# Binary cross-entropy with 8-bit targets on one core: slots of 15232 columns, a larger first chunk, tail chunks loaded in turn, and whole-chunk clip, logarithm and negation

## The chip, the cores and the metric

The kernel runs on one core of one Trainium2 chip. The metric is the device time of one execution in microseconds (us). Times of the same kernel are taken in several runs; a profiled execution adds a trace with the start and the length of every instruction and every DMA packet. The engines that matter here are DVE (VectorE), ACT (ScalarE), POOL (GpSimd, which in this kernel only issues DMAs) and SP (SyncE, which issues the last stores). The core's 16 DMA engines move the data.

## The reference

Inputs are `pred` and `target`, both 8192 x 8192 in fp32; targets are 0 or 1.

```python
eps = 1e-7
pred = np.clip(pred, eps, 1 - eps)
return -(target * np.log(pred) + (1 - target) * np.log(1 - pred))
```

Both inputs are 268.4 MB, and so is the output. Since a target is 0 or 1, the kernel takes one logarithm an element: -ln|target - 1 + pred| is -ln(pred) for target 1 and -ln(1 - pred) for target 0.

## The kernel before, in words

The 67,108,864 elements are seen as one flat array, cut into chunks that are 128 partitions high and `w` columns wide. A chunk of `w` columns is contiguous in memory, and each partition holds one contiguous row of 4w bytes. There are 524288 columns in all: a first chunk of 5120 (chunk 0), 33 chunks of 15360 (`WIDE`, chunks 1 to 33), and a tail of three chunks of 5632, 5632 and 1024. In the code `z` is the number of the last wide chunk, 33; the tail is `z + 1`, `z + 2`, `z + 3`, here also called a, b and c.

Predictions lie in `ring_p`, three slots of 15360 fp32 columns; chunk k uses slot k mod 3, and the tail shares one slot. All work is done in place there, and the result is stored from there. Targets lie in `ring_t`, which has one slot of 15360 columns of 8 bits: the DMA reads fp32 from HBM and writes uint8. So targets k+1 can be loaded only when the merge of chunk k has read targets k.

A chunk goes through these steps, each a helper with a line of its own in the profile:

- `load_p` (L70): the prediction's DMA, from POOL's queue (chunk 0 from ACT's)
- `load_t` (L73): the target's DMA, from POOL's queue
- `clip` (L85): DVE TENSOR_SCALAR, max and min with the two bounds
- `merge`: DVE SCALAR_TENSOR_TENSOR (L91), target - 1 + pred, then on ACT the absolute value (L94) and the logarithm (L95)
- `negate` (L99): DVE TENSOR_SCALAR, times -1
- `store` (L79): the result's DMA, from POOL's queue up to chunk z - 1, from SP's queue from chunk z on. The last chunk's store is cut into three DMAs of 108, 12 and 8 rows

The order of instructions on every engine is written out by hand (`tc.manual_schedule()`); waits between engines follow from the data. An engine takes its instructions strictly in the order of the program, so an instruction that waits holds up all behind it on that engine, and the same holds for the DMA issues of POOL and SP. In an iteration of the main loop, clip, merge and negate work on two halves of a chunk (7680 columns each): merge of both halves of chunk k, the issue of targets k+1, negation of both halves, clip of both halves of chunk k+1, the issue of store k, the issue of predictions k+2. The last iteration issues the predictions of all three tail chunks there. After the loop chunk z is merged, the three target loads of the tail are issued, and the tail's steps are interleaved with the negation of chunk z.

Of the kernel before, what the change touches and what calls it, by code (L numbers as in the profile page):

```python
# [1 line left out]

# [4 lines left out]

EPS = 1e-7

WIDE = 15360  # L10
SLOTS = 3
TAIL = (5632, 5632, 1024)
ROWS = (108, 12, 8)


@with_exitstack
def kernel(
    ctx: ExitStack,
    tc: tile.TileContext,
    pred: bass.AP,  # L20
    target: bass.AP,
    out: bass.AP,
):
    nc = tc.nc
    fp32 = mybir.dt.float32
    low = mybir.dt.uint8
    Alu = mybir.AluOpType
    Act = mybir.ActivationFunctionType
    P = nc.NUM_PARTITIONS

    R, C = pred.shape
    total = R * C // P
    rest = total - sum(TAIL)
    n = rest // WIDE
    first = rest - n * WIDE
    assert 0 < first <= WIDE and n > 4 and sum(TAIL) <= WIDE
    spots = [(first, 0)]
    spots += [(WIDE, k % SLOTS * WIDE) for k in range(1, n + 1)]
    c = (n + 1) % SLOTS * WIDE
    for w in TAIL:  # L40
        spots.append((w, c))
        c += w
    n = len(spots)
    z = n - 1 - len(TAIL)
    starts = [sum(w for w, _ in spots[:k]) * P for k in range(n)]

    pool = ctx.enter_context(tc.tile_pool(name="rings", bufs=1))
    ring_p = pool.tile([P, SLOTS * WIDE], fp32, name="ring_p", tag="ring_p")
    ring_t = pool.tile([P, WIDE], low, name="ring_t", tag="ring_t")
    warm = pool.tile([1, 8], fp32, name="warm", tag="warm")  # L50

    def chunk(ap, k):
        flat = ap.rearrange("r c -> (r c)")
        w = spots[k][0]
        return flat[starts[k] : starts[k] + w * P].rearrange("(p w) -> p w", p=P)

    def cols(ring, k, part, c):
        w = spots[k][0]
        i, m = part
        return ring[:, c + i * w // m : c + (i + 1) * w // m]  # L60

    def p_of(k, part=(0, 1)):
        return cols(ring_p, k, part, spots[k][1])

    def t_of(k, part=(0, 1)):
        return cols(ring_t, k, part, spots[k][1] % WIDE)

    def load_p(k):
        queue = nc.scalar if k == 0 else nc.gpsimd
        queue.dma_start(out=p_of(k), in_=chunk(pred, k))  # L70

    def load_t(k):
        nc.gpsimd.dma_start(out=t_of(k), in_=chunk(target, k))  # L73

    def store(k):
        queue = nc.sync if k >= z else nc.gpsimd
        r = 0
        for rows in ROWS if k == n - 1 else (P,):
            queue.dma_start(out=chunk(out, k)[r : r + rows, :], in_=p_of(k)[r : r + rows, :])  # L79
            r += rows  # L80
        assert r == P

    def clip(k, *part):
        p = p_of(k, *part)
        nc.vector.tensor_scalar(  # L85
            out=p, in0=p, scalar1=EPS, scalar2=1 - EPS, op0=Alu.max, op1=Alu.min
        )

    def merge(k, *part):
        p, t = p_of(k, *part), t_of(k, *part)  # L90
        nc.vector.scalar_tensor_tensor(  # L91
            out=p, in0=t, scalar=1.0, in1=p, op0=Alu.subtract, op1=Alu.add
        )
        nc.scalar.activation(out=p, in_=p, func=Act.Abs)  # L94
        nc.scalar.activation(out=p, in_=p, func=Act.Ln)  # L95

    def negate(k, *part):
        p = p_of(k, *part)
        nc.vector.tensor_scalar(out=p, in0=p, scalar1=-1.0, scalar2=None, op0=Alu.mult)  # L99

    halves = (0, 2), (1, 2)
    tail = range(z + 1, n)
    with tc.manual_schedule():
        load_p(0)
        load_t(0)
        load_p(1)
        nc.vector.memset(warm, 1.0)  # L107
        nc.scalar.activation(out=warm, in_=warm, func=Act.Ln)  # L108
        for h in halves:
            clip(0, h)  # L110
        for k in range(z):
            for h in halves:
                merge(k, h)
            load_t(k + 1)
            for h in halves:
                negate(k, h)
            for h in halves:
                clip(k + 1, h)
            store(k)
            for j in (k + 2,) if k + 2 <= z else tail if k + 2 == z + 1 else ():  # L120
                load_p(j)
        for h in halves:
            merge(z, h)
        for j in tail:
            load_t(j)
        negate(z, halves[0])
        for j in tail:
            clip(j)
        merge(z + 1)
        negate(z, halves[1])  # L130
        store(z)
        merge(z + 2)
        negate(z + 1)
        store(z + 1)
        merge(z + 3)
        negate(z + 2)
        store(z + 2)
        negate(z + 3)
        store(z + 3)


# [1 line left out]
_INS = ['pred', 'target']  # L143
_OUTS = [((8192, 8192), 'float32')]


# [23 lines left out]
```

## Time and profile before

| what | us |
|---|---|
| median of 3 runs (lowest to highest) | 1877.95 (1876.52 to 1878.27) |
| the profiled execution's own time | 1878.45 |
| its span, from the first to the last instruction | 1876.2 |
| DVE busy | 1116.7 |
| ACT busy | 900.3 |
| POOL busy | 277.6 |
| merge on DVE, 7680 columns, one | 8.154 |
| clip or negation on DVE, 7680 columns, one | 4.158 and 4.160 |
| absolute value or logarithm on ACT, 7680 columns, one | 6.595 and 6.603 |

All 16 DMA engines together moved data at a busy share of 9 tenths or more in 39 of 40 equal slices of the span. The DMA issues on POOL take 0.53 us at the least and 4.09 us at the most.

In the views, a line of the timeline gives the start and the length in us, the engine, the line of the kernel, the operation, the names it writes and reads, how often it follows in a row, and in brackets how long the engine sat idle before it and what ended that. POOL's DMA_DIRECT2D is the issue of a DMA (the writing of its descriptors), not the transfer. In a line of the stretches of time, the length of the stretch is followed by the busy time of DVE, ACT and POOL, the granted clock, the DMA's busy share and the GB/s that it moved. A line of the chain of waits gives a start, a length and what the chain went through in that time.

### The profile page before, as it was taken

The numbers are of one execution on the slowest core, as the hardware profiler recorded it, in microseconds if no ns is written. First come the engines' busy times: TensorE is split into PE (matmuls) and PEld (weight loads), VectorE is DVE, ScalarE is ACT, GpSimd is POOL, SyncE is SP. The second block draws the span as 40 slices with busy tenths as digits, with TensorE's granted clock in tenths as the row PEclk, the third lists the DMA queues.
The fourth block names the chain that finished last, engine by engine and source line by source line (L and its number), as shares of the span: only waits on it lengthen the run. The fifth ranks groups of instructions, "written<-read, shape, count | busy, mean of one in ns | idle before, by whom it ended". The sixth has DMA issues, their size and how long they took to land.

```text
span 1876.2 us, 663 instructions
## 1 busy us (share of the span) xinstructions
DVE 1116.7 (60%) x214; ACT 900.3 (48%) x144; POOL 277.6 (15%) x110
## 2 busy tenths in 40 slices
DVE  4566665565566556556655655666566566655655
ACT  2555333555543355553335555444455544445554
POOL 0011111110111111011111101111111011111100
DMA  9999999999999999999999999999999999999998
GB/s 274 271 351 341 309 299 312 303 339 360 347 309 307 309 301 333 361 354 312 313 303 307 319 360 359 324 307 309 307 312 351 360 340 305 309 308 309 338 334 314
DMA packets 16004, 604.02 MB, mean 322 GB/s; under 512 B 1792, under 2 KB 1920, under 8 KB 2560
## 3 DMA queue, kind: packets, MB, share of 16 engines
q0 software_dynamic: 15264, 587.21, 97.6%
q1 hardware_dynamic: 592, 14.16, 1.8%
q10 hardware_dynamic: 144, 2.62, 0.4%
q14 instruction: 4, 0.03, 0.0%
HBM read 536.87 MB, written 268.44 MB: 429 GB/s over the span
## 4 chain that ended last, share of the span: by engine, by line
DMA 67%; issue 28%; DVE 2%; ACT 2%; POOL 0%; POOLq 0%; DVEq 0%; PEldq 0%
DMA ring_t<-in_target_dram 67%; DVE ring_p L91 2%; ACT ring_p L95 1%; ACT ring_p L94 1%; DVE ring_p L99 0%; POOL ring_p L70 0%; POOL out_dram L79 0%; DVEq L165 0%; POOLq L73 0%; POOLq L79 0%; DVEq L91 0%; PEldq L165 0%
## 5 line engine op out<-in xcount | busy, mean ns | idle before, releaser
L94 ACT ACTIVATE ring_p<-ring_p 128x7680 f32<-128x7680 f32 (+3 forms) x71 | 450.8, 6349 | 954.1 <-DVE ring_p L91 954.1
L91 DVE SCALAR_TENSOR_TENSOR ring_p<-ring_t,ring_p 128x7680 f32<-128x7680 uint8 (+3 forms) x71 | 554.3, 7846 | 251.4 <-DMA ring_t<-in_target_dram 251.4
L99 DVE TENSOR_SCALAR ring_p<-ring_p 128x7680 f32<-128x7680 f32 (+3 forms) x71 | 284.3, 4006 | 470.6 <-ACT ring_p L95 470.6
L95 ACT ACTIVATE ring_p<-ring_p 128x7680 f32<-128x7680 f32 (+3 forms) x71 | 451.3, 6356 | 2.3
L85 DVE TENSOR_SCALAR ring_p<-ring_p 128x7680 f32<-128x7680 f32 (+3 forms) x71 | 281.3, 4003 | 19.9 <-DMA ring_p<-in_pred_dram 19.9
L79 POOL DMA_DIRECT2D out_dram<-ring_p x33 | 125.1, 3791 | 711.5 <-DVE ring_p L99 711.5
L73 POOL DMA_DIRECT2D ring_t<-in_target_dram x37 | 19.7, 532 | 818.8 <-DVE ring_p L91 818.1
L70 POOL DMA_DIRECT2D ring_p<-in_pred_dram x36 | 132.9, 3692 | 0.0
L108 ACT ACT_TABLE_LOAD x1 | 1.3, 1283 | 1.1 <-PEq L154 1.1
L107 DVE MEMSET warm<- 1x8 f32 x1 | 0.1, 65 | 0.8 <-PEq L154 0.8
L108 ACT ACTIVATE warm<-warm 1x8 f32<-1x8 f32 x1 | 0.2, 207 | 0.0
L154 POOL MEMSET const-float32-0.0<- 128x1 f32 x1 | 0.1, 98 | 0.2 <-issue 0.2
L154 POOL MEMSET const-bfloat16-1.0<- 128x1 bf16 x1 | 0.1, 101 | 0.0
L154 POOL MEMSET const-float32-1.0<- 128x1 f32 x1 | 0.1, 98 | 0.0
L154 POOL MEMSET const-uint8-127<- 128x1 uint8 x1 | 0.1, 98 | 0.0
## 6 DMA issues: line engine op xcount, KB each, us to landing
ring_p<-in_pred_dram POOLq DMA_DIRECT2D x33, 7680.0 KB, 47.6
out_dram<-ring_p POOLq DMA_DIRECT2D x32, 7680.0 KB, 33.4
ring_t<-in_target_dram POOLq DMA_DIRECT2D x33, 1920.0 KB, 37.8
out_dram<-ring_p SPq DMA_DIRECT2D x1, 7680.0 KB, 19.7
ring_p<-in_pred_dram POOLq DMA_DIRECT2D x2, 2816.0 KB, 37.5
out_dram<-ring_p SPq DMA_DIRECT2D x2, 2816.0 KB, 16.0
ring_p<-in_pred_dram ACTq DMA_DIRECT2D x1, 2560.0 KB, 13.3
out_dram<-ring_p POOLq DMA_DIRECT2D x1, 2560.0 KB, 30.0
```

The source lines that it names most:

```text
L70: queue.dma_start(out=p_of(k), in_=chunk(pred, k))
L73: nc.gpsimd.dma_start(out=t_of(k), in_=chunk(target, k))
L79: queue.dma_start(out=chunk(out, k)[r : r + rows, :], in_=p_of(k)[r : r + rows, :])
L85: nc.vector.tensor_scalar(out=p, in0=p, scalar1=EPS, scalar2=1 - EPS, op0=Alu.max, op1=Alu.min)
L91: nc.vector.scalar_tensor_tensor(out=p, in0=t, scalar=1.0, in1=p, op0=Alu.subtract, op1=Alu.add)
L94: nc.scalar.activation(out=p, in_=p, func=Act.Abs)
L95: nc.scalar.activation(out=p, in_=p, func=Act.Ln)
L99: nc.vector.tensor_scalar(out=p, in0=p, scalar1=-1.0, scalar2=None, op0=Alu.mult)
L107: nc.vector.memset(warm, 1.0)
L108: nc.scalar.activation(out=warm, in_=warm, func=Act.Ln)
L154: nc = _bacc.Bacc("TRN2", target_bir_lowering=False, num_devices=1)
```

## The change

The slots become 15232 columns wide, and the tail 6208, 6208 and 1024. There are again 33 wide chunks; what is left for chunk 0 is 8192 columns. `merge` no longer takes the logarithm; a new helper `log` does. The clip becomes one instruction a chunk everywhere. Logarithm and negation become one instruction a chunk too, but for chunk 1 and chunk z, which keep halves. In the tail, the predictions' loads move behind the merges of chunk z in the program, and each is followed by its targets' load, so POOL issues p(a), t(a), p(b), t(b), p(c), t(c). The tail's steps get a new order: the second negation and the store of chunk z come ahead of all merges of the tail, and the negation of a stays behind the merge of b, that of b behind the merge of c.

```diff
-WIDE = 15360
+WIDE = 15232
 SLOTS = 3
-TAIL = (5632, 5632, 1024)
+TAIL = (6208, 6208, 1024)
...
         nc.scalar.activation(out=p, in_=p, func=Act.Abs)
+
+    def log(k, *part):
+        p = p_of(k, *part)
         nc.scalar.activation(out=p, in_=p, func=Act.Ln)
...
-        for h in halves:
-            clip(0, h)
+        clip(0)
         for k in range(z):
             for h in halves:
                 merge(k, h)
+                if k == 1:
+                    log(k, h)
             load_t(k + 1)
-            for h in halves:
-                negate(k, h)
-            for h in halves:
-                clip(k + 1, h)
+            if k == 1:
+                for h in halves:
+                    negate(k, h)
+            else:
+                log(k)
+                negate(k)
+            clip(k + 1)
             store(k)
-            for j in (k + 2,) if k + 2 <= z else tail if k + 2 == z + 1 else ():
-                load_p(j)
+            if k + 2 <= z:
+                load_p(k + 2)
         for h in halves:
             merge(z, h)
-        for j in tail:
+            log(z, h)
+        a, b, c = range(z + 1, n)
+        for j in a, b, c:
+            load_p(j)
             load_t(j)
         negate(z, halves[0])
-        for j in tail:
-            clip(j)
-        merge(z + 1)
+        clip(a)
         negate(z, halves[1])
         store(z)
-        merge(z + 2)
-        negate(z + 1)
-        store(z + 1)
-        merge(z + 3)
-        negate(z + 2)
-        store(z + 2)
-        negate(z + 3)
-        store(z + 3)
+        merge(a)
+        log(a)
+        clip(b)
+        merge(b)
+        log(b)
+        negate(a)
+        store(a)
+        clip(c)
+        merge(c)
+        log(c)
+        negate(b)
+        store(b)
+        negate(c)
+        store(c)
```

More of the change, by code (lines that the diff above doesn't have):

```diff
@@ L101 @@
     halves = (0, 2), (1, 2)
-    tail = range(z + 1, n)
     with tc.manual_schedule():
```

## The prediction

> **What bounds the kernel now.** I read the page first, then the time by shape, the timeline of the first 120 us and the last 130 us, narrow windows, and the chain in order of time. The page:
>
> ```profile
> DVE 1116.7 (60%) x214; ACT 900.3 (48%) x144; POOL 277.6 (15%) x110
> ...
> DMA  9999999999999999999999999999999999999998
> ...
> HBM read 536.87 MB, written 268.44 MB: 429 GB/s over the span
> ```
>
> No engine is full; the DMA is, in every slice. The chain shows its pace:
>
> ```profile
> 171.89 38.10 DMA ring_t<-in_target_dram
> ...
> 226.60 38.43 DMA ring_t<-in_target_dram
> ...
> 281.65 38.14 DMA ring_t<-in_target_dram
> ...
> 991.84 37.69 DMA ring_t<-in_target_dram
> ...
> 1698.32 37.73 DMA ring_t<-in_target_dram
> ...
> 1752.66 37.76 DMA ring_t<-in_target_dram
> ```
>
> One chunk's target load is issued per line. The last two stand 54.34 us apart, and in a chunk 3 x 7.864 MB cross HBM (prediction in, target in, result out): 434 GB/s, so a transfer of 15360 columns takes 18.12 us, 1.180 ns a column, whatever its kind. From 171.89 to 991.84 fifteen periods average 54.66, 0.32 over that; from there on nothing is over. The packet records show why: at first the sixteen DMA engines pass from one transfer to the next almost together, and the last target rows then take 0.3 to 0.5 us too long; later they have drifted 3 us apart and the rows take 2.28 us throughout.
>
> The bytes don't change, so the change can act only on time in which the DMA does nothing or is slow. It does nothing in two places:
>
> ```profile
> 93.49 8.23 DVE L85 TENSOR_SCALAR ring_p<-ring_p 128x7680 f32<-128x7680 f32 x2
> 93.87 3.89 POOL L79 DMA_DIRECT2D out_dram<-ring_p  x1 [21.99 <-DVE ring_p L99]
> 97.76 4.09 POOL L70 DMA_DIRECT2D ring_p<-in_pred_dram  x1
> ```
>
> ```profile
> 95.00:96.00 1.00, 1.00 (x1) 0.00 (x0) 1.00 (x1) 1.00 0.00 0
> 96.00:97.00 1.00, 1.00 (x1) 0.00 (x0) 1.00 (x1) 1.00 0.00 0
> 97.00:98.00 1.00, 1.00 (x2) 0.00 (x0) 1.00 (x2) 1.00 0.00 0
> ```
>
> (The column before the last is the DMA's share.) Store 1 is late, and the DMA waits some 3.8 us, until 98.3. Why is its issue 3.89 us long where others take 0.53? It ends with the first clip half (93.49 + 4.16 = 97.65), the next issue with the second: **while DVE runs a TENSOR_SCALAR, POOL's issue stands still until that instruction ends.** Beside a SCALAR_TENSOR_TENSOR it does not (0.53 us at 1798.97). The Trainium skill, "SBUF — State Buffer", says of this that VectorE and GpSimd share a port pair, that a two-port VectorE instruction holds it to its end, and that GpSimd can't write DMA descriptors meanwhile; these rows agree, and by that rule one long clip is worse than two short ones.
>
> The other place is the end: the loads finish near 1837.5 and store z (chunk 33) starts at 1841, after its negation:
>
> ```profile
> 1835.80 4.15 DVE L99 TENSOR_SCALAR ring_p<-ring_p 128x7680 f32<-128x7680 f32 x1
> ...
> 1839.98 23.13 SPq L79 DMA_DIRECT2D out_dram<-ring_p  x6
> ```
>
> **Durations.** By shape, 2560 against 7680 columns: TENSOR_SCALAR 1.489 and 4.158 us, so 0.15 + 0.521 ns a column; SCALAR_TENSOR_TENSOR 2.818 and 8.154, 0.15 + 1.042; ACTIVATE 2.33 and 6.60, 0.20 + 0.833. So 15232 columns cost 8.09 (clip, negation) and 12.89 (Ln); 7616: 8.09 (merge), 6.55 (ACT); 6208: 3.39, 6.62, 5.37. Transfers: 15232 columns 17.97, 8192 9.66, 6208 7.32, 1024 1.21. An instruction fewer saves 0.15 to 0.20 us on engines that are 60% and 48% busy: nothing, the DMA hides it.
>
> **Steady loop.** T is the landing of targets k. Merges end at T+16.1, the second Abs at 22.7, the whole Ln at 35.6, the whole negation at 43.7. Store k is released 0.3 later, when clip k+1 already runs: its issue waits for the clip's end, 51.75, and the first bytes move 0.7 later (97.65 to 98.3 above), at T+52.4. Before, the same point was T+43.6 (1779.1 + 0.6, from T = 1736.1). Targets k+1 leave the slowest DMA engine at 53.9 - 0.4 = T+53.5. So 1.1 us of cover is left where there were over ten: no stall on the slowest engine, but an engine that is further ahead now waits. The drift of 3 us can't form, and I take the 0.32 us a period to stay for all 30 periods from chunk 3 on: 9.6 us where 15 x 0.32 = 4.8 was paid. Bounds: the drift forms after all (4.8), or the engines are held so close that 0.8 is paid (24).
>
> **Start.** The first prediction and target share the DMA: 2 x (9.66 - 6.04) = 7.2 us more. Prediction 0 lands at 14.0 + 7.2 = 21.2, clip to 25.7, merges to 34.4, Abs 38.0, Ln 45.1, negation 49.5, clip 1 to 57.6 holding store 0 until 58.3. Targets 1 end at 16.0 + 7.2 + 2 x 18 = 59.2 on the slowest engine: no stall. Chunk 1 lands at 59.7 to 60.7; with logarithm and negation in halves (k == 1) its second negation ends 39 us later, at 99, clip 2 at 107, and store 1 moves at 107.3. The DMA, with 9.66 + 2 x 17.97 of work from some 59 on, runs dry at 105: 2.5 us lost, not 3.8. From there to targets z are 31 stores, 31 predictions and 31 targets. Before: 98.3 + 93 x 18.12 + 0.4 = 1783.9, and the merge of z starts at 1790.51: 6.6 us of slow rows, 4.8 as above and 1.8 in the first periods. After: 107.3 + 93 x 17.97 + 0.4 + 9.6 + 1.8 = 1790.3 = Tz.
>
> **End, from Tz.** Loads a, b, c now run p, t, p, t behind store z-1: store to 17.6, p(a) 24.9, t(a) 32.2, p(b) 39.5. In POOL's order p(b) is now behind t(a), which waits for the first merge of z (Tz+8.4), and p(c) behind t(b), which waits for the second (16.5); each is issued over 20 us before the DMA reaches it, so these waits cost nothing (0.5 us an issue if the DMA stood empty). Clip a (Tz+26 to 29) lies in the gap of DVE before the second negation of z. On ACT Abs, Ln, Abs, Ln end at 34.4; negation to 38.6; store z moves at 39.5 (0.9 after, as at 1839.98), 11 us sooner than before (Tz+50.4): the idle spot is filled. But **store z on SP's queue now meets t(b), just beginning on POOL's.** Each DMA engine has 8 rows of each: a row of store z is 60928 bytes (2.25 us), one of t(b) 24832 (0.92). How two queues share is seen at the start only, there with equal rows: prediction 0, 6.04 us of work, needs 13.3 us to land beside target 0,
>
> ```profile
> ring_p<-in_pred_dram ACTq DMA_DIRECT2D x1, 2560.0 KB, 13.3
> ```
>
> and the packets alternate one by one. I take row by row here too: t(b) ends 39.5 + 7.3 + 7 to 8 x 2.25 = 63 to 64. All loads and store z end at 67.2. Behind t(b): merge b 64 to 70.6, and **neg(a) stands behind merge b on DVE**, though Ln(a) was done at 56.0: neg(a) to 73.9, store a at 74.9. The DMA idles 67.2 to 74.9. Ln(b) ends at 81.4, neg(b) 84.85, store b 85.8 to 93.1, again 3.6 idle; chunk c and the end 3.0 later (1873.2 to 1876.2): Tz+96.1, before Tz+85.7.
>
> The Trainium skill, "DMA: Bandwidth & Descriptors", section "Queues, rings and completion order", has each engine go round its queue rows by whole packets of several descriptors; with store rows first that would put t(b) at 64 to 65 as well, and the sum within 1 us.
>
> **Sum.** 1790.3 + 96.1 = 1886.4 of span. The profiled execution took 1878.45 for a span of 1876.2: 2.25 more, 1888.6. It lies 0.5 above the median 1877.95, within the runs (1876.52 to 1878.27 and this one). Forecast 1888.5.
>
> **Rivals.**
> - **Equal shares by bytes (not slower).** t(b) gets half the DMA and lands at 39.5 + 14.6 + 0.4 = 54.5. Merge b to 61.2, neg(a) 64.5, store a queued before store z is done, 74.5; neg(b) 75.4, store b 76.3 to 83.6; end Tz+86.7: 1879.3, and 1874.5 if the drift forms too. It decides at t(b)'s landing: before Tz+56 the DMA stays nearly full. For: the start rows fit both rules; against: alternation by packet is what they show directly. Chance 0.2.
> - **Loads first.** t(b) lands at 47, end Tz+84.3: 1876.9, with the drift 1872. Against: the 13.3 us. Chance 0.08.
> - **Engines held close.** 0.8 a period: 1903. For: right after the idle spot at 98, with all engines in step, two changes of transfer cost 1.0 and 1.2 us; against: the excess fell to 0.3 in two periods. Chance 0.12.
> - **The issue doesn't wait through the long clip.** Then store k is ready at T+44.7, the drift forms, and the gap of 2.5 us goes: 1888.5 - 4.8 - 2.5 = 1881, the end as forecast. The rows at 93.49 speak against it; counted with the forecast.
>
> **How the numbers follow.** Forecast (row by row, 1881 to 1896): 0.6. About 0.2% (3.8 us, 1874.2 to 1881.7) is what a measurement here can tell from no change. Faster takes loads first with the drift, or equal shares with a little more: 0.12. Same: the rest of equal shares and loads first, 0.16. Slower: 0.6 + 0.12 = 0.72. Range 1874 to 1900: equal shares at the low end, half of the held case at the high one.
>
> **What would show it.** POOL's store issues near 7.8 us instead of 3.9; periods of 54.2 (54.34 x 15232/15360 + 0.32) to the end; DMA share 0 near 106; t(b) landing 24 us after p(b); DVE idle ahead of merge b for some 15 us; a DMA hole ahead of store a and of store b. Wrong if t(b) lands within 16 us of p(b), or the periods fall to 53.9.

## The result and the profile after

The changed kernel takes 1890.49 us (median of 6 runs, 1887.74 to 1894.21) against 1877.49 us (6 runs, 1876.52 to 1879.08): ratio 1.0069, 95% interval 1.0056 to 1.0082, so 13.0 us slower. The profiled execution has a span of 1889.9 us, before 1876.2. The page:

```profile
DVE 1109.2 (59%) x148; ACT 897.3 (47%) x112; POOL 296.8 (16%) x110
...
DMA  9999999999999999999999999999999999999997
...
HBM read 536.87 MB, written 268.44 MB: 426 GB/s over the span
```

DVE and ACT have 7.5 and 3.0 us less to do, and that is worth nothing: the same bytes cross HBM, at 426 GB/s instead of 429. The 13.7 us of span lie in two stretches. I cut at Tz, the start of the first merge of chunk z: Tz is 1794.7 (before 1790.5), and the end comes 95.1 us later (before 85.7).

The start, from the timeline, and one stretch of 1 us (the column before the last is the DMA's share):

```profile
97.25 8.09 DVE L85 TENSOR_SCALAR ring_p<-ring_p 128x15232 f32<-128x15232 f32 x1
97.63 7.83 POOL L79 DMA_DIRECT2D out_dram<-ring_p  x1 [21.81 <-DVE ring_p L102]
105.37 16.09 DVE L91 SCALAR_TENSOR_TENSOR ring_p<-ring_t,ring_p 128x7616 f32<-128x7616 uint8 x2
105.44 0.53 POOL L70 DMA_DIRECT2D ring_p<-in_pred_dram  x1
```

```profile
105.00:106.00 1.00, 0.96 (x2) 0.00 (x0) 0.97 (x2) 1.00 0.00 0
```

POOL's issue of store 1 stands through the whole clip, 7.83 us; the next issue, beside a merge, takes 0.53. A stretch counts the whole time of a row where the row starts, so the length of the hole is read from the packet records: ahead of store 1 the sixteen DMA engines stand idle for 2.0 us in the mean, 1.6 of them all at once; before it was 3.7 in the mean.

The loop, from the chain of waits (one target load a line):

```profile
669.54 37.47 DMA ring_t<-in_target_dram
...
723.49 39.75 DMA ring_t<-in_target_dram
...
779.72 37.34 DMA ring_t<-in_target_dram
...
833.54 37.80 DMA ring_t<-in_target_dram
```

Periods of 53.95, 56.23 and 53.82: 17 of the 30 periods from chunk 3 on stay within 0.3 us of the DMA's pace (54.34 x 15232/15360 = 53.89), the others lose up to 2.3 us, and unlike before this goes on to the end. The mean over the 30 periods from chunk 3 to chunk z is 54.40.

The end, from the timeline, with stretches of 2 us:

```profile
1833.21 47.79 SPq L79 DMA_DIRECT2D out_dram<-ring_p  x6
...
1845.16 5.38 ACT L98 ACTIVATE ring_p<-ring_p 128x6208 f32<-128x6208 f32 x1
1856.74 6.63 DVE L91 SCALAR_TENSOR_TENSOR ring_p<-ring_t,ring_p 128x6208 f32<-128x6208 uint8 x1 [13.72 <-DMA ring_t<-in_target_dram]
1863.28 3.39 DVE L102 TENSOR_SCALAR ring_p<-ring_p 128x6208 f32<-128x6208 f32 x1
```

```profile
1862.00:1864.00 2.00, 2.00 (x2) 0.60 (x1) 0.00 (x0) 1.00 0.18 16
1864.00:1866.00 2.00, 2.00 (x1) 2.00 (x1) 0.00 (x0) 1.00 0.00 0
1866.00:1868.00 2.00, 1.97 (x3) 2.00 (x1) 0.00 (x0) 1.00 0.46 199
...
1876.00:1878.00 2.00, 2.00 (x2) 0.22 (x1) 0.00 (x0) 1.00 0.00 0
```

DVE stands idle 13.72 us until t(b) lands, because store z (issued at 1833.21) shares the DMA with it. Then everything has been loaded and nothing is ready to store: two holes, ahead of store a and of store b.

### The profile page after: what moved, and what is told of

It reads as the page before. It is cut to its first block, busy times and chain, and to the rows that moved or that the text cites. A ratio compares the mean times of both kernels' runs of the same rounds, so it can differ in the third digit from the quotient of the medians.

```text
span 1889.9 us, 528 instructions
## 1 busy us (share of the span) xinstructions
DVE 1109.2 (59%) x148; ACT 897.3 (47%) x112; POOL 296.8 (16%) x110
## 4 chain that ended last, share of the span: by engine, by line
DMA 67%; issue 27%; DVE 3%; ACT 2%; POOL 0%; POOLq 0%; DVEq 0%
DMA ring_t<-in_target_dram 66%; DVE ring_p L91 2%; DMA ring_p<-in_pred_dram 1%; ACT ring_p L98 1%; ACT ring_p L94 1%; DVE ring_p L102 0%; POOL out_dram L79 0%; DVE ring_p L85 0%; DVEq L178 0%; POOL ring_p L70 0%; POOLq L73 0%; POOLq L79 0%; DVEq L91 0%
## 5 line engine op out<-in xcount | busy, mean ns | idle before, releaser
L94 ACT ACTIVATE ring_p<-ring_p 128x7616 f32<-128x7616 f32 (+3 forms) x71 | 451.3, 6356 | 976.5 <-DVE ring_p L91 976.5
L102 DVE TENSOR_SCALAR ring_p<-ring_p 128x15232 f32<-128x15232 f32 (+4 forms) x39 | 279.2, 7162 | 647.1 <-ACT ring_p L98 647.1
L91 DVE SCALAR_TENSOR_TENSOR ring_p<-ring_t,ring_p 128x7616 f32<-128x7616 uint8 (+3 forms) x71 | 554.3, 7847 | 101.6 <-DMA ring_t<-in_target_dram 101.5
L98 ACT ACTIVATE ring_p<-ring_p 128x15232 f32<-128x15232 f32 (+4 forms) x39 | 444.8, 11406 | 1.2
L79 POOL DMA_DIRECT2D out_dram<-ring_p x33 | 258.2, 7826 | 876.8 <-DVE ring_p L102 876.8
L85 DVE TENSOR_SCALAR ring_p<-ring_p 128x15232 f32<-128x15232 f32 (+3 forms) x37 | 278.7, 7533 | 19.5 <-DMA ring_p<-in_pred_dram 19.5
L70 POOL DMA_DIRECT2D ring_p<-in_pred_dram x36 | 19.0, 528 | 0.0
```

The source lines that it names most:

```text
L85: nc.vector.tensor_scalar(out=p, in0=p, scalar1=EPS, scalar2=1 - EPS, op0=Alu.max, op1=Alu.min)
L91: nc.vector.scalar_tensor_tensor(out=p, in0=t, scalar=1.0, in1=p, op0=Alu.subtract, op1=Alu.add)
```

## The experiments

Three theories were put to the test. **End**: store z beside t(b) costs the end about 10 us. **Clip**: the long clip holds POOL's issue, the late store holds the DMA engines in step, and that brings the slow rows of the loop (mine). **Rivals for the loop**: the sizes, or the whole logarithm and negation. All runs at a glance; "period" is the mean of the 30 periods from chunk 3 to z (from the starts of the first merges), "end" what follows Tz, both of the profiled execution; the kernel before had medians of 1877.4 to 1877.9 beside them:

| run | median us | ratio to before, 95% interval | period | end |
|---|---|---|---|---|
| before | 1877.49 | | 54.50 | 85.7 |
| after | 1890.49 | 1.0069 (1.0056 to 1.0082) | 54.40 | 95.1 |
| e1_clip_halves | 1888.32 | 1.0055 (1.0043 to 1.0068) | 54.39 | 94.2 |
| e2_neg_a_first | 1891.26 | 1.0069 (1.0056 to 1.0081) | 54.36 | 97.7 |
| e3_store_z_pool | 1880.71 | 1.0012 (1.0003 to 1.0020) | 54.30 | 86.8 |
| e4_store_z_pieces | 1887.59 | 1.0050 (1.0036 to 1.0064) | 54.23 | 93.9 |
| e4b_pieces_late | 1881.25 | 1.0016 (1.0007 to 1.0025) | 54.40 | 86.6 |
| e5_before_whole_clip | 1882.46 | 1.0036 (1.0025 to 1.0047) | 54.48 | 85.7 |
| e6_before_whole_log | 1887.55 | 1.0055 (1.0042 to 1.0067) | 54.83 | 85.7 |
| e7_sizes_only | 1872.03 | 0.9970 (0.9959 to 0.9981) | 54.00 | 89.4 |
| e9_pred_ahead | 1882.36 | 1.0024 (1.0014 to 1.0035) | 54.16 | 95.5 |
| e10_halves_z_pool | 1867.74 | 0.9945 (0.9933 to 0.9958) | 54.10 | 83.5 |
| e11_halves_z_pool_ahead | 1871.44 | 0.9968 (0.9956 to 0.9981) | 54.18 | 86.8 |
| e12_pred_late | 1880.18 | 1.0015 (1.0006 to 1.0024) | 54.58 | 85.7 |

A period without any slow row is 54.34 with the old size (before, e5, e6, e12) and 53.89 with the new one.

### The end: store z on POOL's queue

```diff
-        queue = nc.sync if k >= z else nc.gpsimd
+        queue = nc.sync if k > z else nc.gpsimd
```

> The changed kernel with store z on POOL's queue, behind the tail's loads, instead of SP's beside them. Mine (store z takes the DMA from t(b) row by row): t(b) lands some 47 us after the first merge of z instead of 62, merge b starts right after clip b, store b starts 10 us sooner, end 10 us sooner: 1880.5. Rival (the order on DVE or the later store costs it): not more than 2 us, 1888.5 or over.

Measured 1880.71, 9.8 us less than after; the end falls from 95.1 to 86.8. The timeline of this run:

```profile
1830.53 0.54 POOL L79 DMA_DIRECT2D out_dram<-ring_p  x1 [20.76 <-DVE ring_p L102]
...
1840.55 6.62 DVE L91 SCALAR_TENSOR_TENSOR ring_p<-ring_t,ring_p 128x6208 f32<-128x6208 uint8 x1 [0.48 <-DMA ring_t<-in_target_dram]
...
1847.62 3.39 DVE L102 TENSOR_SCALAR ring_p<-ring_p 128x6208 f32<-128x6208 f32 x1 [0.44 <-ACT ring_p L98]
```

Store z is issued as early as after (Tz+38.7 here, Tz+38.5 there), but queued behind the loads; merge b starts at Tz+48.8 instead of Tz+62.0 and waits 0.48 us for t(b) instead of 13.72. So the collision costs the end 8.3 of its 95.1 us.

### The end: smaller rows of store z

```diff
+        if k == z:
+            w = spots[k][0]
+            for i in range(4):
+                s = slice(i * w // 4, (i + 1) * w // 4)
+                queue.dma_start(out=chunk(out, k)[:, s], in_=p_of(k)[:, s])
+            return
```

> The changed kernel with store z on SP as it is, cut into four DMAs of a quarter of the columns each (rows of 15232 bytes, 0.56 us, in place of 60928, 2.25 us). If the two queues take turns by rows, five rows of t(b) are left when store z starts and each waits for 0.56 us instead of 2.25: t(b) ends about 8.5 us sooner, merge b starts 8.5 to 10 us sooner, 1881. If they share by bytes, or go by several rows at a time, t(b) lands as before and the time stays at 1890.

Measured 1887.59: a miss, and the timeline says why:

```profile
1814.46 13.83 SPq L81 DMA_DIRECT2D out_dram<-ring_p  x4
...
1837.42 3.40 DVE L91 TENSOR_SCALAR ring_p<-ring_p 128x6208 f32<-128x6208 f32 x1 [3.43 <-DMA ring_p<-in_pred_dram]
...
1849.45 6.62 DVE L97 SCALAR_TENSOR_TENSOR ring_p<-ring_t,ring_p 128x6208 f32<-128x6208 uint8 x1 [8.63 <-DMA ring_t<-in_target_dram]
```

A quarter needs only the half of the negation that wrote it, so the first two left at 1814.46, 13 us ahead of the rest, and slowed p(b) too (clip b waits for it at 1837.42). An estimate made after the run, from the row times above: taking turns by rows from Tz+26 on, 16 rows of 0.56 us beside 16 load rows of 0.92 end p(b) at Tz+48.5, and the 6 to 7 rows of t(b) left then end at Tz+59.5; equal shares by bytes would give Tz+52.6 and Tz+65. In the packet records p(b) is complete at Tz+48.0 and t(b) at Tz+59.9; clip b starts at Tz+48.4, merge b at Tz+60.4. The run with the last quarter issued first mends the expectation's flaw:

```diff
-            for i in range(4):
+            for i in (3, 2, 1, 0):
```

> Store z in four DMAs of a quarter of the columns as in the run before, but the last quarter is issued first, so that all four wait for the second negation of z (in the run before, the first two quarters left 12 us earlier and met p(b) and t(b) both). If the queues take turns row by row, t(b) has some five rows left when the store starts, each waits for a row of 0.56 us instead of 2.25: merge b starts near Tz+51 instead of Tz+62 (Tz is the first merge of chunk z), the end comes 9 us sooner, 1881.5. If they share by bytes, t(b) lands near Tz+51 to 55 with whole rows too, which the run after has refuted; if the store goes first as a whole, merge b stays at Tz+62 and the time at 1890.

```profile
1832.97 1.90 SPq L81 DMA_DIRECT2D out_dram<-ring_p  x4
...
1846.62 6.63 DVE L97 SCALAR_TENSOR_TENSOR ring_p<-ring_t,ring_p 128x6208 f32<-128x6208 uint8 x1 [3.85 <-DMA ring_t<-in_target_dram]
```

All four leave at 1832.97 (Tz+38.5), merge b starts at Tz+52.1, and the time is 1881.25, 9.2 less than after. The same store on the same queue at the same moment holds t(b) up for 10 us less when its rows are a quarter as long. In the packet records of after, too, store rows and target rows alternate one by one on each DMA engine. Five or six rows of store z go ahead of t(b) there; at 2.25 - 0.56 = 1.69 us less a row that is 8.5 to 10.1 us, measured 62.0 - 52.1 = 9.9. The DMA does not share by bytes.

### The end: the order on DVE

```diff
         clip(b)
+        negate(a)
+        store(a)
         merge(b)
         log(b)
-        negate(a)
-        store(a)
```

> The changed kernel with the negation and the store of a ahead of the merge of b. Mine, from the trace after: b sets the end (merge b waits for t(b), then Abs, Ln, negation, store), and it is not touched, so the DMA hole ahead of store a closes, the one ahead of store b grows by as much, and the time stays at 1890 within 1.5 us. Rival (the negation of a standing behind the merge of b costs the hole of 7 us): 1883.

Measured 1891.26 against 1890.49, the runs' ranges overlap. The timeline:

```profile
1849.16 3.39 DVE L102 TENSOR_SCALAR ring_p<-ring_p 128x6208 f32<-128x6208 f32 x1 [7.55 <-ACT ring_p L98]
1857.89 6.62 DVE L91 SCALAR_TENSOR_TENSOR ring_p<-ring_t,ring_p 128x6208 f32<-128x6208 uint8 x1 [5.34 <-DMA ring_t<-in_target_dram]
```

The negation of a runs 14 us sooner and nothing is won: merge b still waits for t(b), and what follows b sets the end.

### The loop: the long clip

```diff
-            clip(k + 1)
+            for h in halves:
+                clip(k + 1, h)
```

> The changed kernel with the clip of the main loop in two halves again, nothing else. Mine (the long clip holds POOL's issue of the store, and the store released late keeps the DMA engines in step): the issue falls from 7.83 to 4.0 us, the store is released at T+48.4 instead of T+52.4, the cover grows from about 1 to 5 us, the engines drift apart, and the periods fall from the measured 54.40 mean to 53.9 to 54.1; store 1 moves near 102 and the DMA no longer runs dry there (2 us). Together 10 us off: 1877 to 1884. Rival (the slow rows come at every change of transfer, held or not): only the 2 us at store 1, about 1888.5.

A store's issue in this run:

```profile
1019.53 3.86 POOL L79 DMA_DIRECT2D out_dram<-ring_p  x1 [27.11 <-DVE ring_p L102]
```

Measured 1888.32, 2.2 less than after, and a period of 54.39: the rival's number. The runs' ranges overlap, but the trace shows the same: no gap ahead of store 1, and the first merge of chunk 3 comes 2.4 us sooner. The issue of the store does fall to 3.86 us, and by the packet records the DMA engines do drift 2.3 us apart and stay so, while after they fall back to 0.5 us again and again; the slow rows stay. **The theory of the clip falls**: the loop has its slow rows without it. The long clip on the kernel before, by itself:

```diff
-            for h in halves:
-                clip(k + 1, h)
+            clip(k + 1)
```

> The kernel before with one clip instruction a chunk in the main loop, nothing else. Both theories: store 1 waits through the whole clip (8.2 instead of 4.1 us), and the DMA hole near 95 grows from 3.8 to 7.8 us: 1881.5. Theory of the late store (a store released late holds the DMA engines in step and brings slow rows): the release moves from T+43.6 to T+47.7, 6 us of cover are left, periods as before, 54.50: 1881.5. Theory of sizes (slow rows come with the chunk's size): the same 1881.5. If the long clip costs something in every chunk, 1886 or more.

The issue of store 1 in this run:

```profile
93.10 7.89 POOL L79 DMA_DIRECT2D out_dram<-ring_p  x1 [22.00 <-DVE ring_p L99]
```

Measured 1882.46, 5.1 more than before, but the nine runs fall into two groups: five from 1880.72 to 1882.46 and four from 1886.15 to 1888.71. The profiled execution (1880.83) is of the lower group. In it the first merge of chunk 3 is 3.3 us later, by the longer hole at the start, and the periods are 54.48 as before (54.50): there the loop pays nothing for a long clip. Where the upper group loses 5 us more no trace shows, and a cost of the long clip in the loop is not excluded for it.

### The loop: the whole logarithm and negation, and the sizes

On the kernel before, `merge` without the logarithm, and in the loop

```diff
             for h in halves:
                 merge(k, h)
+                if k == 1:
+                    log(k, h)
             load_t(k + 1)
-            for h in halves:
-                negate(k, h)
+            if k == 1:
+                for h in halves:
+                    negate(k, h)
+            else:
+                log(k)
+                negate(k)
```

> The kernel before with logarithm and negation in one instruction a chunk (halves for chunks 1 and z, as in the change), clips in halves, old sizes. Release of the store at T+48.8, 5 us of cover. Theory of sizes: no change, periods 54.50, 1877.5. Theory that the lateness of the whole logarithm brings the slow rows (the run with clips in halves still had them): periods near 54.34 + 0.49 = 54.83, 10 us more, 1887.

Measured 1887.55, 10.2 more than before, periods 54.83: the second theory, to the number. Its chain and its timeline:

```profile
1048.81 37.74 DMA ring_t<-in_target_dram
...
1103.17 38.81 DMA ring_t<-in_target_dram
...
1158.59 37.68 DMA ring_t<-in_target_dram
...
1212.88 38.64 DMA ring_t<-in_target_dram
```

```profile
1068.22 8.16 DVE L102 TENSOR_SCALAR ring_p<-ring_p 128x15360 f32<-128x15360 f32 x1 [19.70 <-ACT ring_p L98]
...
1076.68 3.89 POOL L79 DMA_DIRECT2D out_dram<-ring_p  x1 [27.34 <-DVE ring_p L102]
1080.56 4.09 POOL L70 DMA_DIRECT2D ring_p<-in_pred_dram  x1
```

Periods of 54.36, 55.42 and 54.29 in turn, every second one an excess of 1.1. The packet records show no gap between targets and store in the later loop; the last rows of stores and of targets are slow, by up to 0.6 us in the mean of the sixteen, with the engines 2.5 us apart. The store's descriptors are written at T+48.3 (before 42.9), those of the next predictions at T+52.4 (before 47.0). The sizes by themselves:

```diff
-WIDE = 15360
+WIDE = 15232
 SLOTS = 3
-TAIL = (5632, 5632, 1024)
+TAIL = (6208, 6208, 1024)
```

> The kernel before with the new sizes alone (15232; 6208, 6208, 1024; first chunk 8192). The DMA hole near 95 closes (3.8 us), and the end comes 88.7 us after the first merge of z instead of 85.7, since the tail is larger. Theory of sizes: periods of 53.89 + 0.49 = 54.38 throughout, 1882. Theory of the late whole logarithm: periods of 53.89 + 0.17 = 54.06, 1872.5.

Measured 1872.03, **5.3 less than before** (0.9970, 0.9959 to 0.9981): the hole at the start closes (the packet records show no gap ahead of store 1), and the periods are 54.00, 0.11 over the pace. Sizes bring no slow rows.

The packet records tell what the rest of the change adds to such a period (means of the sixteen engines). From this run to the changed kernel (54.00 to 54.40), the rows of predictions and stores take 0.31 us longer and those of targets no longer, and the engines stand idle 0.11 us more. From the kernel before to the one with the whole logarithm and negation (54.50 to 54.83), predictions and stores take 0.22 us longer and targets 0.10, with no more idle time. So most of the loss is in slow rows, and the engine that is ahead and has to wait, which I had forecast, is the small part.

### The loop: what of the whole instructions costs

Two runs asked whether it is the lateness of the DMA issues. In the first, the changed kernel issues predictions k+2 ahead of store k:

```diff
             load_t(k + 1)
+            if k + 2 <= z:
+                load_p(k + 2)
...
             store(k)
-            if k + 2 <= z:
-                load_p(k + 2)
```

> The changed kernel with the load of predictions k+2 issued right after targets k+1, ahead of store k, in POOL's order. The instructions on DVE and ACT stay whole. The DMA then always has a prediction's load queued behind the targets when the store is released, 18 us more cover, and no hole near 105. Theory of late descriptors (the whole logarithm brings slow rows because store k and predictions k+2 are queued only when the DMA engines are about to need them): slow rows go, periods near 53.9 to 54.0, 12 to 16 us off: 1876. Rival (the whole instructions themselves bring the slow rows by when they run): periods stay near 54.4, and only the hole goes: 1887.5.

Measured 1882.36, 8.1 less than after, periods 54.16: between the two theories. In the second, on the kernel before, only the predictions' issue becomes late:

```diff
-            for h in halves:
-                clip(k + 1, h)
+            clip(k + 1, halves[0])
+            clip(k + 1, *(() if k > 1 else (halves[1],)))
```

> The kernel before, but from chunk 3 on the second clip instruction covers the whole chunk instead of its second half (the first half is clipped twice, which changes nothing in the data). The store's descriptors are written at T+42.9 as before, those of predictions k+2 only at the end of the longer instruction, T+51 instead of T+47; logarithm, negation and the store's time are untouched. If predictions queued late bring the slow rows (in the run with the whole logarithm alone they were queued at T+52.4, and periods were 54.83): periods 54.7 to 54.9, 1885 to 1889. If not (the late store, or ACT's and DVE's whole instructions): 54.5 and 1877.5.

```profile
850.39 3.89 POOL L79 DMA_DIRECT2D out_dram<-ring_p  x1 [21.99 <-DVE ring_p L99]
854.27 8.20 POOL L70 DMA_DIRECT2D ring_p<-in_pred_dram  x1
```

The issue is late as wanted (8.20 instead of 4.09 us), but the time is 1880.18 and the periods 54.58: 0.08 more than before, where the whole logarithm brings 0.33. So predictions that are late alone (written by T+51.1 here, T+52.4 there) bring about a quarter of it.

### A version that beats both

New sizes, the changed tail with store z on POOL's queue, and all of the loop in halves:

```diff
             for h in halves:
                 merge(k, h)
-                if k == 1:
-                    log(k, h)
+                log(k, h)
             load_t(k + 1)
-            if k == 1:
-                for h in halves:
-                    negate(k, h)
-            else:
-                log(k)
-                negate(k)
-            clip(k + 1)
+            for h in halves:
+                negate(k, h)
+            for h in halves:
+                clip(k + 1, h)
```

> New sizes and the changed kernel's tail, with clip, logarithm and negation of the main loop in halves and store z on POOL's queue. Start and loop as in the run with the sizes alone (first merge of z at 1779.8), end as in the run with store z on POOL (86.8 later): 1869. If the parts don't add, over 1873.

Measured 1867.74, 10.1 less than the runs of before beside it (1877.88), ratio 0.9945 (0.9933 to 0.9958), and 22.8 less than after. The sum came out better than its parts: Tz is 2.7 us later than expected (1782.5, periods 54.10 for 54.00), and the end 3.3 us shorter (83.5 for 86.8). From this kernel to after, the parts measured one by one are 9.8 for store z on SP's queue, 2.2 for the whole clip and 10.2 for the whole logarithm and negation, 22.2 in all, so they add on the new sizes as well. Its DMA row on the page has no slice under 9 tenths:

```profile
DMA  9999999999999999999999999999999999999999
```

With the predictions ahead of the stores as well:

> As the run before it, with the predictions' load ahead of the store as well. Theory of late descriptors: in halves the store was early enough already, so little is left to win: the first periods' slow rows of some 3 us at most, 1866 to 1869. Rival: the same 1869.

Measured 1871.44: a miss, 3.7 more than without. Its periods are 54.18, those of the same order with whole instructions 54.16: **in that order whole or halves makes no difference**, which speaks for a cost through the order and time of the DMAs and not through the running of the whole instructions; but the order has slow rows of its own, 0.27 to 0.29 a period.

## Why the prediction came out right

The forecast was 1888.5, the median is 1890.49. The end, which gave all of the forecast slowdown, came as worked out; the loop did not, and that the number is only 2.0 off is in part luck. By its steps:

- **The bound.** Right: every run is the DMA's pace plus what the DMA loses. Fewer and longer instructions gained nothing.
- **POOL's issue and the long clip.** Right: 7.83 us for a forecast of 7.8, and "the issue doesn't wait through the long clip" is refuted. The port pair shared by VectorE and GpSimd, in the Trainium skill's "SBUF — State Buffer", section "Who interferes with whom", fits all runs: 3.86 to 3.89 beside half a clip, 7.82 to 7.92 beside a whole one, 0.53 beside a merge.
- **Start.** Right within 1.3 us: store 1 moves at 106.0, forecast 107.3; the hole is 2.0 us in the mean of the engines, forecast 2.5. The last rows of targets 1, which took 3.54 us in the mean before, took 2.26.
- **Steady loop.** The term was mis-sized, and its cause was wrong. Forecast 30 periods of 0.32 over the pace, 9.6 us; measured 54.40 - 53.89 = 0.51, 15 us. The step that failed is "the drift of 3 us can't form, and I take the 0.32 us a period to stay". The first half holds: in the changed kernel the engines fall back to 0.5 us apart. The second does not follow from it: with the clip in halves the drift forms and the slow rows stay (54.39), and the long clip on the kernel before adds none in the execution that was traced (54.48 for 54.50). What brings them is the whole logarithm and negation (54.83 on the kernel before, 10.2 us). I had taken them into account only as time until the store is released, with 5 us of cover left in that run, and so would have priced that edit alone at nothing.
- **End.** Right: Tz+95.1 for Tz+96.1, by rows taking turns. t(b) is complete 22 us after p(b), forecast 24; merge b starts at Tz+62.0, forecast 64. Inside, one error made up for part of another. The first rows of store z move at Tz+42.0 to 43.7 and not at 39.5, so three or four of t(b)'s eight rows are through by then, and five or six rows of store z go ahead of t(b), not seven or eight. But the last of these turns, which I had not counted, comes after the data: t(b)'s last row ends at Tz+59.3, and the 4-byte record that completes the load stands behind one more row of store z, until Tz+61.6. The DMA is then idle for 4.2 us ahead of store a (forecast 7.7) and 3.4 ahead of store b (3.6). That the negation of a stands behind merge b is true and costs nothing: b sets the end either way.
- **Rivals.** Equal shares by bytes: refuted by merge b at Tz+62.0, where they gave 54.5, and by the runs with store z in pieces. Loads first: refuted by the 13.72 us. Engines held close: they are held close, but the loss is 0.51 a period and not 0.8, and with the engines apart (clip in halves) it is as large. That one edit could make the kernel faster (the sizes, 5.3 us) is in the working (the hole near 95), but I did not price it by itself.
- **Sum.** Loop 5.7 too little, start 1.3 and end 1.0 too much: the span is 3.5 short (1886.4 for 1889.9), the forecast 2.0 below the median. The profiled execution (1891.86), to which these steps belong, lies 1.4 above the median; the forecast is 3.4 short of it.

By runs, the change comes apart as: sizes -5.3, whole clip +2.2 (in the changed kernel, where the ranges overlap; 3.4 to 11.3 on the kernel before), whole logarithm and negation +10.2, the new tail +5.7 (end 95.1 against 89.4 with the same sizes, from one trace each); -5.3 + 2.2 + 10.2 + 5.7 = 12.8, measured 13.0. The parts were measured on different kernels, so that they add to within 0.2 is closer than they are known.

**What stays open:** how the whole logarithm and negation bring slow rows. Shown is that it needs neither the long clip nor the new sizes nor engines in step, that predictions late alone bring about a quarter of it, and that in another order of the DMAs whole instructions and halves cost the same. A store and predictions that are late together, as in those runs, were not tried with halves, and the whole logarithm and the whole negation were never tried apart. Open too is the upper group of runs with the long clip on the kernel before.

## What to carry to other kernels

When the DMA is the bound, as here, an instruction saved on DVE or ACT is worth nothing, and one that ends later can cost much: look at what it does to the time at which the next transfers are queued. A store issued earlier, on another queue, took the DMA from a load that the end waited for (13.72 us); behind the loads on the same queue the wait was 0.48 us. Take a change apart edit by edit: here one part was 5.3 us faster and hidden by the others.

## What the runs showed of the hardware

- Two DMA queues took turns by rows, though their rows differ in size: store rows of 60928 bytes beside target rows of 24832 held up t(b) until Tz+62.0, rows of 15232 bytes until Tz+52.1. The Trainium skill, "DMA: Bandwidth & Descriptors", section "Queues, rings and completion order", speaks of turns by whole packets of several descriptors; in these packet records each turn is one row.
- The 4-byte record that completes a load takes a turn as well. Behind t(b)'s last data row it waited for one more row of the store: 2.26 us in after (Tz+59.3 to 61.6), 0.56 with rows a quarter as long (Tz+51.1 to 51.7).
- The last row of a store or of a target load can take 0.3 to 1 us longer than its 2.25 us when the DMA engines go on to the next transfer, without any of them idle; predictions followed by targets hardly showed it. In the kernel with the whole logarithm it came in every second chunk (periods 54.36 and 55.42). I did not expect that, and no run here settles it.
- Two issues that wait on POOL while DVE runs TENSOR_SCALARs get one gap between instructions each: the store 3.89 us, the predictions behind it 4.09, or 8.20 when the next instruction is twice as long.
